# A two-layer hybrid attention trunk: probabilities turned square by square on VectorE, and sums of log f formed by scans

## The chip, the cores and the metric

The kernel runs on one core of one Trainium2 chip. The metric is the device time of one launch in microseconds (us). The kernel before was run three times: 934.83, 939.86 and 940.43 us, median 939.86 us. One further execution was profiled; all durations below are of that one.

## The reference

The input x is 256 rows of 2048 numbers in fp32. Each of two layers normalises x, multiplies it by one input projection, feeds four groups of four heads, gates each group, and adds an output projection to x. A last normalisation ends it.

```python
def hybrid_layer(x, l, ...):
    h = rms_norm(x, norm_g)
    p = split_columns(h @ w_in)
    log_f = log_sigmoid(p["fox_f"] + fox_fb)
    fox  = softmax(q k^T / sqrt(d) + F[t] - F[s]) v * silu(g)      # F = cumsum(log_f), causal
    diff = rms_norm((softmax(q1 k1^T) - lam * softmax(q2 k2^T)) v) * silu(g)
    moba = softmax(q k^T / sqrt(d)) v * silu(g)     # 256 rows are one block: plain causal attention
    a = log_sigmoid(p["gla_a"] @ wa2 + ba) / 16     # per head and channel
    gla  = rms_norm(o) * silu(g)                    # o_t = q_t S_t, S_t = diag(exp a_t) S_{t-1} + k_t^T v_t
    return x + concat(fox, diff, moba, gla) @ w_out
```

## The kernel before

**Projections.** All projections run on TensorE in fp32r with every operand split in a high and a low part (hi x hi, lo x hi, hi x lo), into the PSUM tiles `mm`. The weights come in 300 steps. A step loads a tile `raw` (128x1024, 512 KB, on SP's queue), ScalarE writes its high part `hi` and VectorE its low part `lo` (both line 183, `hi_of` and `lo_of`), and TensorE multiplies 12 times (line 285): 8 with `hi`, then 4 with `lo`. There are four buffers each of `raw`, `hi` and `lo`, and the builder prepares a step three steps ahead of its products (`ahead`, line 1249): the parts of step i+3 can be written when TensorE has left those of step i-1. Layer 0 has steps 0 to 119 of the input projection and 120 to 151 of the output projection; layer 1 likewise from 152. `hTp` is the turned, normalised x; `mTh` and `mTl` are the turned outputs of the groups, high and low. The output projection takes the groups in the order gla, fox, diff, moba, two steps each, so that its seventh and eighth step (126 and 127, 278 and 279) are the first to need moba.

**Side work.** Everything else is written as Python generators in a list of tasks (`tick`, line 266). After each step every task may go on to its next `yield`. `give_time` (line 1242) adds the step's TensorE time to a budget of VectorE and one of ScalarE, and `Costed` (line 171) charges each of their instructions a fixed cost and a cost per element. While either budget is overdrawn, no task goes on (line 270). When a step needs what no task has yet made, the tasks go on regardless, and the step's products are written behind what they wrote (line 1290). The order that results is fixed before the launch, and each engine runs its own list in order.

**Turned probabilities.** A softmax leaves its probabilities with the queries across the partitions: `p0`, four heads of 128x128 (first 128 queries), and `p1`, eight such squares (last 128 queries, two halves of keys). The product with the values needs them turned. `turned_p` (line 773) calls `turned` (line 292): two VectorE transposes write a tile `six` (128x1536), in which each 32x32 block is turned in place, and `moved` (line 305) sends it to DRAM (`turn`) by one DMA of POOL's queue and back by four, which puts the blocks where they belong. Five more turns of the task list are let pass (`LAND`). Fox and moba (`attend_columns`, line 791) read `six` directly; diff (line 905), where it is the stationary operand, first copies it to `z0` and `z1` on ScalarE. This happens six times: fox, diff and moba in two layers. All other tiles that are turned (queries, keys, gates, x) go the same way by `turned`.

**Sums of log f.** Gated linear attention (`gla`, line 622) needs exp of sums of log f over ranges of rows, for seven levels of halving and the two halves (NL + 1 = 8 sets of 128 columns, `ee`, tile `eight`). Log f is made with the rows across the partitions (`gl`), split in `gh` and `glo`, and multiplied by a constant 0/1 matrix divided by 16 (`a_r`, 128x1152): for each of two head pairs and two halves of rows, `a_r` gives a PSUM tile `pe`, of which ScalarE takes exp into `ee`. There are 10 products for each pair, 40 in all. Then come products of queries with `ee` (`tq`), of `ee` with keys, the score products `side<-tq,eight`, and masked copies.

Of the kernel before, what the change touches and what calls it, by code (L numbers as in the profile page):

```python
# [21 lines left out]
P = 128  # L22
# [4 lines left out]
H = 4  # L27
# [12 lines left out]
T2 = 5  # L40
T6 = 1
# [23 lines left out]
def _constants():  # L65
# [20 lines left out]
    sets, masks = [], []  # L86
    for h in GLA_LEVELS:
        blk, second = i // (2 * h), (i // h) % 2 == 1
        ref = blk * 2 * h + h - 1
        u, t = i[:, None], i[None, :]  # L90
        a = np.where(second[None, :], (u > ref[None, :]) & (u <= t), (u > t) & (u <= ref[None, :]))
        sets.append(a / GLA_TAU)
        masks.append(((blk[:, None] == blk[None, :]) & ~second[:, None])[:, second])
    sets += [(i[:, None] > i[None, :]) / GLA_TAU, (i[:, None] <= i[None, :]) / GLA_TAU]
    put("sets", np.concatenate(sets, 1), "b")
# [117 lines left out]
def hybrid_trunk(  # L213
# [17 lines left out]
    v_ = Costed(nc.vector, 0.06, 1.05e-3)  # L231
# [15 lines left out]
    s6 = Slots(wk, "six", T6)  # L247
# [85 lines left out]
    a_r = cp.tile([P, (NL + 2) * P], F32R, name="a_r")  # L333
# [24 lines left out]
    def constants():  # L358
# [6 lines left out]
        for name in ("sets", "upto", "masks"):  # L365
# [12 lines left out]
        v_.tensor_copy(a_r, s[0])  # L378
        v_.tensor_copy(upto_r, s[1])
        v_.tensor_copy(masks.rearrange("p l t -> p (l t)"), s[2])  # L380
# [241 lines left out]
    def gla(l, an):  # L622
# [14 lines left out]
        gl = yield from s2.take([P, 2, 256])  # L637
        yield from log_sigmoid(gl.rearrange("p m e -> p (m e)"), al[:, :512], e)
# [18 lines left out]
        for pair in range(2):  # L657
            ee = yield from s8.take([P, 2, NL + 1, P])
            for m in range(2):
                pe = yield from take_side()  # L660
                for b in range(2):
                    for part in (gh, glo):
                        lhs = part[:, m, pair * P:(pair + 1) * P]
                        if b == 0:
                            matmul(pe[:, :512], lhs, a_r[:, 0:512], part is gh, part is glo)
                        elif m == 0:
                            matmul(pe[:, 512:], lhs, a_r[:, 512:1024], part is gh, part is glo)
                        else:
                            matmul(pe[:, 512:896], lhs, a_r[:, 512:896], part is gh, False)
                            matmul(pe[:, 896:], lhs, a_r[:, (NL + 1) * P:], False, part is glo)  # L670
# [3 lines left out]
            yield  # L674
# [19 lines left out]
            v_.tensor_mul(ee[:, 1, NL], ee[:, 1, NL], qv[:, 1])  # L694
            both = yield from take_both()
# [21 lines left out]
        s2.put(gh, glo)  # L717
# [55 lines left out]
    def turned_p(p0, p1, pool0=s2, slot0=None):  # L773

        def release():
            pool0.put(p0 if slot0 is None else slot0)
            s4.put(p1)

        return (yield from turned([p0, p1.rearrange("p h j s -> p (h j) s")], s6, release))

    def normalised(p0, p1, su):
# [7 lines left out]
        return (yield from turned_p(p0, p1))  # L789

    def attend_columns(l, gi, name, qT, kT, forget=None):
# [11 lines left out]
        for h in range(H):  # L803
            v0, v1 = vn[:, 0, h * P:(h + 1) * P], vn[:, 1, h * P:(h + 1) * P]
            matmul(o[:, h, :P], v0, t[:, :, h], True, True)
# [524 lines left out]
```

## Time and profile before

| | us |
|---|---|
| three runs | 934.83, 939.86, 940.43 |
| profiled execution | 932.37 |
| its span, from the first to the last instruction | 930.2 |
| TensorE busy in the span | 913.7 |
| VectorE busy | 577.4 |
| ScalarE busy | 505.3 |
| GpSimd busy | 104.0 |

The profile names engines PE (TensorE's products), PEld (its loads of stationary operands), DVE (VectorE), ACT (ScalarE), POOL (GpSimd) and SP. An fp32 product of 128x128 stands in it as two instructions, so 12 such products are a group of x24. Line 183 is the helper that charges the budgets and line 285 the helper that issues products: there the tiles tell what an instruction is. Numbers behind a tile's name tell buffers apart and are left out by the profile.

### The profile page before, as it was taken

To read this page: it belongs to the slowest core of one execution; us is meant where nothing else is said; L and a number is where in the kernel's file an instruction comes from. 1 tells how busy PE (TensorE), PEld (TensorE's weight loads), DVE (VectorE), ACT (ScalarE), POOL (GpSimd) and SP (SyncE) were. 2 spreads that over 40 slices of the span, in tenths; PEclk is the share of its full clock that TensorE was granted. 3 is DMA by queue.
4 is the path that set the end of the run, shared out by engine and by line. 5 is a ranking of instruction groups with operands and counts; after the bars stand their busy time and mean duration, and the time that the engine had idled before them with its cause. 6 is when DMAs were issued, how large, how long until landed. Compare 5 with 4: busy or idle time off the path is not lost.

```text
span 930.2 us, 12655 instructions
## 1 busy us (share of the span) xinstructions
PE 913.7 (98%) x4734; PEld 777.7 (84%) x4734; DVE 577.4 (62%) x782; ACT 505.3 (54%) x712; POOL 104.0 (11%) x174
## 2 busy tenths in 40 slices
PE   9999999999999999999999999999999999989996
PEld 7989888898888888788898888888878888868886
DVE  7663876674764576456845457866656655664563
ACT  7587654455644456455656566446355445744441
POOL 0010011210111122001200101012201112130000
PEclk9999999999999999999999999999999999999999
DMA  9766476787677768678856856578956887695652
GB/s 324 268 209 198 163 240 200 233 238 258 216 209 248 239 201 274 204 228 268 261 176 185 245 143 205 181 220 230 284 177 212 249 239 219 201 296 199 199 163 91
DMA packets 59407, 204.56 MB, mean 220 GB/s; under 512 B 8497, under 2 KB 8785, under 8 KB 59346
## 3 DMA queue, kind: packets, MB, share of 16 engines
q1 hardware_dynamic: 46048, 164.20, 55.5%
q0 software_dynamic: 11664, 37.76, 14.7%
q10 hardware_dynamic: 1634, 1.80, 0.6%
q8 instruction: 37, 0.61, 0.3%
q14 instruction: 24, 0.20, 0.1%
HBM read 183.80 MB, written 19.92 MB: 219 GB/s over the span
## 4 chain that ended last, share of the span: by engine, by line
PE 92%; DMA 4%; issue 2%; DVE 1%; ACT 1%; POOL 1%; POOLq 0%; DVEq 0%; SPq 0%; ACTq 0%
PE mm L285 82%; PE side L285 10%; DMA six<-turn 2%; DMA raw<-in_weights 1%; DMA four<-turn 1%; DVE lo L183 0%; DMA four<-in_xt 0%; ACT hi L183 0%; POOL six L312 0%; ACT four L183 0%; DVE xs L183 0%; POOL four L312 0%; PE side L289 0%; DVE four L183 0%; DVE hTp L183 0%
## 5 line engine op out<-in xcount | busy, mean ns | idle before, releaser
L183 DVE TENSOR_TENSOR lo<-raw,hi 128x1024 fp32r<-128x1024 f32 (+3 forms) x301 | 365.7, 1220 | 297.3 <-ACT hi L183 292.7
L183 ACT ACTIVATE hi<-raw 128x1024 fp32r<-128x1024 f32 (+3 forms) x301 | 316.8, 1059 | 366.3 <-PE mm L285 318.0
L285 PE MATMUL mm<-hi,hTp 128*128 128x512 f32 (+2 forms) x2048 | 465.4, 371 | 0.3 <-DVE hTp L183 0.3
L285 PEld LDWEIGHTS mm<-hi,hTp 128*128 128x128 f32 x2048 | 358.2, 188 | 66.2 <-issue 1.4
L285 PE MATMUL mm<-lo,hTp 128*128 128x512 f32 (+2 forms) x1024 | 249.8, 369 | 0.1
L285 PEld LDWEIGHTS mm<-lo,hTp 128*128 128x128 f32 x1024 | 181.1, 188 | 32.9 <-DVE lo L183 0.3
L285 PE MATMUL mm<-hi,mTh 128*128 128x512 f32 (+1 forms) x256 | 95.2, 377 | 0.0
L285 PE MATMUL mm<-hi,mTl 128*128 128x512 f32 (+1 forms) x256 | 95.0, 376 | 0.0
L285 PE MATMUL mm<-lo,mTh 128*128 128x512 f32 (+1 forms) x256 | 64.4, 376 | 0.0
L312 POOL DMA_DIRECT2D four<-turn x84 | 46.0, 554 | 108.5 <-DMA turn<-four 53.9
L285 PEld LDWEIGHTS mm<-hi,mTl 128*128 128x128 f32 x256 | 48.2, 188 | 9.0 <-DVE mTl L183 0.3
L285 PEld LDWEIGHTS mm<-hi,mTh 128*128 128x128 f32 x256 | 48.2, 188 | 8.7
L285 PEld LDWEIGHTS mm<-lo,mTh 128*128 128x128 f32 x256 | 46.2, 188 | 8.8
L309 POOL DMA_DIRECT2D turn<-four x21 | 12.2, 582 | 324.3 <-DVE four L183 324.3
L183 ACT ACTIVATE four<-mm,rstd 128x512 f32<-128x512 f32 (+2 forms) x56 | 33.6, 647 | 3.6 <-DVE fx L183 3.5
L183 ACT ACT_TABLE_LOAD x26 | 33.4, 1283 | 3.3 <-DVE an L183 3.0
L285 PEld LDWEIGHTS side<-four,four 128*128 128x128 f32 (+1 forms) x256 | 26.0, 190 | 3.5 <-issue 1.4
L285 PE MATMUL side<-four,four 128*128 128x128 f32 (+1 forms) x256 | 27.7, 277 | 1.1 <-DMA four<-turn 1.1
L183 DVE STREAM_TRANSPOSE four<-four 128x1024 f32<-128x1024 f32 x18 | 22.3, 1241 | 0.3
L183 ACT ACTIVATE four<-side,nb 128x256 f32<-128x256 f32 (+1 forms) x48 | 20.4, 434 | 1.2 <-DVE nb L183 1.2
L183 DVE COPY_PREDICATED four<-masks,side 128x128 f32<-128x128 uint8 x56 | 19.1, 341 | 1.8
L285 PE MATMUL side<-six,four 128*128 128x128 f32 x96 | 13.1, 301 | 5.4 <-DMA six<-turn 5.4
(146 smaller groups left out, 540.5 us busy)
## 6 DMA issues: line engine op xcount, KB each, us to landing
raw<-in_weights SPq DMA_DIRECT2D x272, 512.0 KB, 4.2
turn<-four POOLq DMA_DIRECT2D x21, 512.0 KB, 4.8
four<-turn POOLq DMA_DIRECT2D x84, 128.0 KB, 4.9
raw<-in_weights SPq DMA_DIRECT2D x16, 516.0 KB, 4.8
raw<-in_weights SPq DMA_DIRECT2D x15, 528.0 KB, 5.0
turn<-six POOLq DMA_DIRECT2D x6, 768.0 KB, 4.5
six<-turn POOLq DMA_DIRECT2D x24, 192.0 KB, 6.6
turn<-gate POOLq DMA_DIRECT2D x4, 512.0 KB, 4.4
```

Of the source, the lines that this page charges most:

```text
L183: return f(*args, **kw)
L285: t_.matmul(out, lhsT, rhs, start=start, stop=stop)
L309: g_.dma_start(via, t.rearrange("p c a b -> p c (a b)"))
L312: g_.dma_start(t[c * 32:(c + 1) * 32].rearrange("p q a b -> p q (a b)"), via[:, c].rearrange("(q i) e -> i q e", q=4))
```

## The change

- `turned_p` no longer goes over DRAM. It writes a fixed tile `pT` (128 x 12 squares x 128) by VectorE transposes that read 32 partitions and write 32 others: for each of four target strips, four source strips, a transpose of `p0` (32 x 4 x 32) and one of `p1` (32 x 8 x 32). Where the source lies above the diagonal, only the second key half of `p1` is not zero there, and one transpose of 32x4x32 is left. That makes 10 of 32x8x32 and 16 of 32x4x32 for each turn, in four portions with a `yield` behind each. `pT` is zeroed once; a turn waits until the products of the one before it have been written.
- `attend_columns` and `diff` read `pT`; the ScalarE copies to `z0` and `z1` are gone. The pool `six` is gone.
- In `gla`, log f is made with head channels across the partitions (the two operands of `side<-wa,at` change places). Four scans (`cum`) for each layer give the running sum. For each pair, seven subtractions of 128x256 give the sum of each row less that of its block's reference row, one subtraction and one copy of 128x128 the last set. ScalarE takes their absolute value and then exp with the scale -1/16, both 128x1024, for each half of rows. The 40 products with `a_r`, the split in `gh` and `glo`, the PSUM tiles `pe` and the constant `a_r` with its load and its cast are gone. A `yield` is added ahead of the score products.
- The charge for a VectorE instruction goes from 0.06 + 1.05 n/1000 to 0.16 + 1.04 n/1000 us (n: elements in a partition).
- The pool `two` (2 KB in a partition) has seven buffers in place of five.

```diff
-T2 = 5
-T6 = 1
+T2 = 7
...
-    v_ = Costed(nc.vector, 0.06, 1.05e-3)
+    v_ = Costed(nc.vector, 0.16, 1.04e-3)
...
-        for m in range(2):
-            matmul(al[:, m * 256:(m + 1) * 256], at17[:, m * P:(m + 1) * P], wa[:, l], True, True)
+        for pair in range(2):
+            matmul(al[:, pair * SEQ:(pair + 1) * SEQ], wa[:, l, pair * P:(pair + 1) * P], at17, True, True)
...
-        gh = yield from s2.take([P, 2, 256], F32R)
-        hi_of(gh, gl)
-        yield
-        glo = yield from s2.take([P, 2, 256], F32R)
-        lo_of(glo, gl, gh)
+        cum = yield from s2.take([P, 2, SEQ])
+        for pair in range(2):
+            for m in range(2):
+                c = slice(m * P, (m + 1) * P)
+                v_.tensor_tensor_scan(cum[:, pair, c], gl[:, pair, c], gl[:, pair, c], 0.0, op0=OP.add, op1=OP.bypass)
...
+            for i, h in enumerate(GLA_LEVELS):
+                src = cum[:, pair].rearrange("p (m b w) -> p m b w", m=2, w=2 * h)
+                v_.tensor_sub(ee[:, :, i].rearrange("p m (b w) -> p m b w", w=2 * h), src,
+                              src[:, :, :, h - 1:h].to_broadcast([P, 2, 64 // h, 2 * h]))
+                if i == 3:
+                    yield
+            v_.tensor_scalar(ee[:, 0, NL], cum[:, pair, :P], cum[:, pair, P - 1:P], None, op0=OP.subtract)
+            v_.tensor_copy(ee[:, 1, NL], cum[:, pair, P:])
+            yield
             for m in range(2):
-                pe = yield from take_side()
...
+                a_.activation(ee[:, m], ee[:, m], AF.Abs)
+                a_.activation(ee[:, m], ee[:, m], AF.Exp, scale=-1.0 / GLA_TAU)
                 yield
-                a_.activation(ee[:, m].rearrange("p l t -> p (l t)"), pe, AF.Exp)
-                side.put(pe)
...
+    def turned_p(p0, p1):
+        while env["pT"] is None:
+            yield
+        t, env["pT"] = env["pT"], None
+        low = p1.rearrange("p h j s -> p (h j) s")
+        for s in range(4):
+            for q in range(4):
+                to, at = slice(s * 32, s * 32 + 32), slice(q * 32, q * 32 + 32)
+                if q < s:
+                    v_.transpose(t[to, H:3 * H:2, at], low[at, 0:2 * H:2, to])
+                else:
+                    v_.transpose(t[to, 0:H, at], p0[at, :, to])
+                    v_.transpose(t[to, H:3 * H, at], low[at, :, to])
+            yield
+        return t
```

How the order of instructions moves is shown at three places; each list is of one engine, in its order.

TensorE in layer 0, in the block of columns of `fox_v` (128x258), where the first set of sums stood. Before (`a_r` is the constant matrix, `two_732` and `two_752` are `gh` and `glo`):

```order
L285 MATMUL mm<-hi,hTp 128x258 x16
L285 MATMUL mm<-lo,hTp 128x258 x8
L285 MATMUL side_916<-a_r,two_732 128x512
L285 MATMUL side_916<-a_r,two_752 128x512
L285 MATMUL side_916<-a_r,two_732 128x512
L285 MATMUL side_916<-a_r,two_752 128x512
L285 MATMUL mm<-hi,hTp 128x258 x16
L285 MATMUL mm<-lo,hTp 128x258 x8
```

and now:

```order
L277 MATMUL mm<-hi,hTp 128x258 x16
L277 MATMUL mm<-lo,hTp 128x258 x8
L277 MATMUL mm<-hi,hTp 128x258 x16
L277 MATMUL mm<-lo,hTp 128x258 x8
L277 MATMUL mm<-hi,hTp 128x512 x8
L277 MATMUL mm<-lo,hTp 128x512 x4
```

The sums' products have left the list, here and at seven more places; nothing takes their place.

VectorE at the end of layer 0's input projection, from moba's turn to its gating. Before (`six_3184` is the tile of turned blocks, `four_3356` the gated result of moba, each `lo` the low part of one step's weights, three or four steps ahead of its products):

```order
L183 STREAM_TRANSPOSE six_3184<-two_3061 128x4x4x32
L183 STREAM_TRANSPOSE six_3184<-four_3089 128x8x4x32
L183 TENSOR_TENSOR lo<-raw,hi 128x1024 x2
L183 TENSOR_TENSOR mTl<-four_3182,mTh 128x1024
L183 TENSOR_TENSOR lo<-raw,hi 128x1024 x6
L183 TENSOR_TENSOR four_3356<-side_3325,gate_3137 128x4x8x32
L183 TENSOR_TENSOR lo<-raw,hi 128x1024 x2
L183 TENSOR_TENSOR mTl<-four_3356,mTh 128x1024
L183 TENSOR_TENSOR lo<-raw,hi 128x1024 x9
```

and now, from the middle of the third of the turn's four portions on:

```order
L176 STREAM_TRANSPOSE pT<-four_3116 32x8x32
L176 STREAM_TRANSPOSE pT<-two_3088 32x4x32
L176 STREAM_TRANSPOSE pT<-four_3116 32x8x32
L176 TENSOR_TENSOR lo<-raw,hi 128x1024
L176 STREAM_TRANSPOSE pT<-four_3116 32x4x32 x3
L176 STREAM_TRANSPOSE pT<-two_3088 32x4x32
L176 STREAM_TRANSPOSE pT<-four_3116 32x8x32
L176 TENSOR_TENSOR lo<-raw,hi 128x1024 x6
L176 TENSOR_TENSOR four_3442<-side_3429,gate_3164 128x4x8x32
L176 TENSOR_TENSOR mTl<-four_3442,mTh 128x1024
L176 TENSOR_TENSOR lo<-raw,hi 128x1024 x8
```

Before, six steps lay between the low part of diff (`mTl<-four_3182`) and moba's gating, and two more between gating and moba's low part; now gating and low part stand side by side, with no step between. On TensorE, moba's product with the values stood behind the third step of the output projection, three steps ahead of the first that needs moba; it now stands behind the sixth, right ahead of it. Layer 1 shows the same.

ScalarE in layer 1, at the exponentials of the first pair of gated linear attention. Before (`eight_4677` is `ee`, `side_4678` and `side_4709` are the sums in PSUM, `fe` belongs to the forget gate of fox):

```order
L183 ACTIVATE hi<-raw 128x1024 x2
L183 ACTIVATE four_4689<-mm,rstd 128x254 x2
L183 ACT_TABLE_LOAD
L183 ACTIVATE eight_4677<-side_4678 128x1024
L183 ACTIVATE hi<-raw 128x1024
L183 ACTIVATE eight_4677<-side_4709 128x1024
L183 ACTIVATE fe<-fx 128x8
L183 ACTIVATE fe<-fe 128x8
L183 ACT_TABLE_LOAD
L183 ACTIVATE fe<-fe 128x8
L183 ACTIVATE hi<-raw 128x1024 x2
```

and now:

```order
L176 ACTIVATE hi<-raw 128x1024
L176 ACTIVATE eight_4722<-eight_4722 128x1024
L176 ACT_TABLE_LOAD
L176 ACTIVATE eight_4722<-eight_4722 128x1024
L176 ACTIVATE fe<-fx 128x8
L176 ACTIVATE fe<-fe 128x8
L176 ACT_TABLE_LOAD
L176 ACTIVATE fe<-fe 128x8
L176 ACTIVATE hi<-raw 128x1024
L176 ACTIVATE eight_4722<-eight_4722 128x1024
L176 ACT_TABLE_LOAD
L176 ACTIVATE eight_4722<-eight_4722 128x1024
L176 ACTIVATE hi<-raw 128x1024 x5
```

Two absolute values and one more load of a table stand between the same copies of weights. The list as a whole has 25 loads of tables, where it had 27.

## Rows read from the trace of the kernel before

**Rows 1.** The first part of the page: busy time of each engine, its share of the span, and its instructions.

```profile
PE 913.7 (98%) x4734; PEld 777.7 (84%) x4734; DVE 577.4 (62%) x782; ACT 505.3 (54%) x712; POOL 104.0 (11%) x174
```

**Rows 2.** The chain of waits that ended last, over the whole span: its shares by engine and line.

```profile
by line: PE mm L285 81.6%; PE side L285 10.0%; issue 1.8%; DMA six<-turn 1.6%; DMA raw<-in_weights 1.3%; DMA four<-turn 0.6%; DVE lo L183 0.5%; DMA four<-in_xt 0.4%; ACT hi L183 0.3%; POOL six L312 0.3%; ACT four L183 0.2%; DVE xs L183 0.2%
```

**Rows 3.** TensorE in order of time, at the three places in the middle of the span where it stood still. Columns: start, duration (us), engine, line, operation, tiles, shape, count, and in brackets the idle time before with what ended it.

```profile
378.70 2.92 PE L285 MATMUL side<-six,four 128*128 128x128 f32 x24 [1.29 <-DMA six<-turn]
...
677.01 1.13 PE L285 MATMUL side<-four,four 64*128 64x128 f32 x14 [1.09 <-DMA four<-turn]
...
837.00 4.54 PE L285 MATMUL side<-six,four 128*128 128x128 f32 x24 [4.12 <-DMA six<-turn]
```

**Rows 4.** Pieces of the chain of waits in order of time (start, us, what): a product of probabilities and values that waited for nothing, and the two that stand at the end of each layer with what each waited for last.

```profile
260.46 2.68 PE side L285 x24
...
372.00 6.56 DMA six<-turn
...
378.70 2.92 PE side L285 x24
...
829.00 7.87 DMA six<-turn
...
837.00 4.54 PE side L285 x24
```

**Rows 5.** Stretches around the two waits at the ends of the layers: busy time of each engine with its instructions, granted TensorE clock, share of the DMA engines, GB/s.

```profile
377.50:382.00 4.50, 3.30 (x27) 3.25 (x28) 1.57 (x2) 0.10 (x1) 0.00 (x0) 1.00 1.00 398
833.00:837.00 4.00, 0.00 (x1) 0.03 (x1) 1.23 (x1) 0.07 (x1) 0.00 (x0) 1.00 1.02 267
837.00:842.00 5.00, 5.00 (x27) 4.92 (x28) 0.42 (x1) 0.00 (x0) 0.00 (x0) 0.66 1.02 401
```

**Rows 6.** TensorE's pieces of the chain in order of time (start, us, what): the sums of log f by products (x4 and x6), the first and the last two of the eight, and one step of projection (x12).

```profile
84.85 0.93 PE side L285 x4
...
88.64 0.99 PE side L285 x6
...
116.20 2.73 PE mm L285 x12
...
571.95 0.93 PE side L285 x4
...
575.61 0.99 PE side L285 x6
```

**Rows 7.** VectorE's groups of instructions, shapes kept apart: line, engine, operation, tiles, shapes, count, then busy us, mean ns of one, then the idle time before them with what ended it.

```profile
L183 DVE TENSOR_TENSOR lo<-raw,hi 128x1024 fp32r<-128x1024 f32 x268 | 325.9, 1221 | 271.6 <-ACT hi L183 267.1 <-PE mm L285 3.9
...
L183 DVE STREAM_TRANSPOSE four<-four 128x1024 f32<-128x1024 f32 x18 | 22.3, 1241 | 0.3
...
L183 DVE TENSOR_TENSOR tq<-eight,four 64x128 f32<-64x128 f32 x56 | 16.0, 286 | 0.6
...
L183 DVE TENSOR_TENSOR eight<-eight,four 128x128 f32<-128x128 f32 x36 | 7.9, 282 | 0.0
...
L183 DVE STREAM_TRANSPOSE six<-four 128x1024 f32<-128x1024 f32 x6 | 7.2, 1202 | 0.0
...
L183 DVE TENSOR_TENSOR two<-four,ct 128x256 f32<-128x256 f32 x8 | 3.3, 416 | 0.0
...
L183 DVE STREAM_TRANSPOSE six<-two 128x512 f32<-128x512 f32 x4 | 2.8, 704 | 0.0
...
L183 DVE TENSOR_SCALAR f<-f 128x8 f32<-128x8 f32 x2 | 0.3, 171 | 0.1
```

**Rows 8.** ScalarE's groups in the same form.

```profile
L183 ACT ACTIVATE hi<-raw 128x1024 fp32r<-128x1024 f32 x268 | 282.3, 1060 | 342.0 <-PE mm L285 303.9 <-DMA raw<-in_weights 10.6 <-DVE six L183 8.8
...
L183 ACT ACT_TABLE_LOAD x26 | 33.4, 1283 | 3.3 <-DVE an L183 3.0
...
L183 ACT ACTIVATE four<-four 128x1024 f32<-128x1024 f32 x10 | 10.5, 1052 | 0.3 <-DVE hTp L183 0.3
...
L183 ACT ACTIVATE eight<-side 128x1024 f32<-128x1024 f32 x8 | 8.2, 1023 | 0.9 <-PE side L285 0.8
...
L183 ACT ACTIVATE four<-six 128x1024 f32<-128x1024 f32 x2 | 2.1, 1043 | 0.0
...
L183 ACT ACTIVATE two<-six 128x512 f32<-128x512 f32 x2 | 1.3, 632 | 4.1 <-DMA six<-turn 4.1
...
L183 ACT ACTIVATE fe<-fe 128x8 f32<-128x8 f32 x4 | 0.8, 208 | 0.1
```

**Rows 9.** VectorE and ScalarE in order of time behind the product at 378.70 us (columns as in rows 3): gating the result, its high part, its low part.

```profile
381.65 1.23 DVE L183 TENSOR_TENSOR four<-side,gate 128x1024 f32<-128x1024 f32 x1 [2.80 <-PE side L285]
...
384.47 1.05 ACT L183 ACTIVATE mTh<-four 128x1024 fp32r<-128x1024 f32 x1
...
388.52 1.22 DVE L183 TENSOR_TENSOR mTl<-four,mTh 128x1024 fp32r<-128x1024 f32 x1
```

**Rows 10.** Pieces of the chain (start, us, what): the products of the first set of gated linear attention, in layer 0 and in layer 1.

```profile
103.33 3.12 PE side L285 x28
...
559.77 3.34 PE side L285 x28
```

**Rows 11.** The list of waits, one row: engine, line and tile that waited, for what; us in total, times, longest.

```profile
DVE lo L183 <- ACT hi L183: 292.7, 199, 5.2
```

**Rows 12.** The tile of turned probabilities: time from the issue of its DMAs to their landing.

```profile
DMA to landing us min/median/max: 4.1/6.4/9.2
```

More of the change, by code (lines that the diff above doesn't have):

```diff
@@ L85, in _constants @@
     put("neg", np.where(i[None, :] > i[:, None], NEG, 0.0), "b")
-    sets, masks = [], []
+    masks = []
     for h in GLA_LEVELS:
         blk, second = i // (2 * h), (i // h) % 2 == 1
[L89 to L92, printed above, removed]
         masks.append(((blk[:, None] == blk[None, :]) & ~second[:, None])[:, second])
-    sets += [(i[:, None] > i[None, :]) / GLA_TAU, (i[:, None] <= i[None, :]) / GLA_TAU]
-    put("sets", np.concatenate(sets, 1), "b")
     put("masks", np.concatenate(masks, 1), "b")
@@ L364, in constants @@
         s = []
-        for name in ("sets", "upto", "masks"):
+        for name in ("upto", "masks"):
             c, n = CAT[name]
@@ L377, in constants @@
         yield
-        v_.tensor_copy(a_r, s[0])
-        v_.tensor_copy(upto_r, s[1])
-        v_.tensor_copy(masks.rearrange("p l t -> p (l t)"), s[2])
+        v_.tensor_copy(upto_r, s[0])
+        v_.tensor_copy(masks.rearrange("p l t -> p (l t)"), s[1])
         v_.tensor_scalar(ones_r, ident, 0.0, 1.0, op0=OP.mult, op1=OP.add)
@@ L632, in gla @@
         al = yield from take_side()
-        for m in range(2):
-            matmul(al[:, m * 256:(m + 1) * 256], at17[:, m * P:(m + 1) * P], wa[:, l], True, True)
+        for pair in range(2):
+            matmul(al[:, pair * SEQ:(pair + 1) * SEQ], wa[:, l, pair * P:(pair + 1) * P], at17, True, True)
         yield
         e = yield from s2.take([P, 512])
-        gl = yield from s2.take([P, 2, 256])
-        yield from log_sigmoid(gl.rearrange("p m e -> p (m e)"), al[:, :512], e)
+        gl = yield from s2.take([P, 2, SEQ])
+        yield from log_sigmoid(gl.rearrange("p x t -> p (x t)"), al[:, :512], e)
         s2.put(e)
@@ L658, in gla @@
             ee = yield from s8.take([P, 2, NL + 1, P])
-            for m in range(2):
-                pe = yield from take_side()
[L661 to L670, printed above, removed]
+            for i, h in enumerate(GLA_LEVELS):
[7 more added lines that the diff above has]
+            yield
+            for m in range(2):
+                a_.activation(ee[:, m], ee[:, m], AF.Abs)
+                a_.activation(ee[:, m], ee[:, m], AF.Exp, scale=-1.0 / GLA_TAU)
                 yield
-                a_.activation(ee[:, m].rearrange("p l t -> p (l t)"), pe, AF.Exp)
-                side.put(pe)
-            yield
             def half(z, h, second):
@@ L771, in softmax @@
         return p
[L773 to L779, printed above, removed]
+    def turned_p(p0, p1):
[11 more added lines that the diff above has]
+                    v_.transpose(t[to, H:3 * H, at], low[at, :, to])
+            yield
+        return t
     def normalised(p0, p1, su):
@@ L788, in normalised @@
         yield
-        return (yield from turned_p(p0, p1))
+        t = yield from turned_p(p0, p1)
+        s2.put(p0)
+        s4.put(p1)
+        return t
     def attend_columns(l, gi, name, qT, kT, forget=None):
@@ L979, in diff @@
         s4.put(p1[1])
-        t = yield from turned_p(p0[:, 0], p1[0], s4, p0)
-        z0 = yield from s2.take([P, H, P])
-        z1 = yield from s4.take([P, 2 * H, P])
-        for z, part in ((z0, t[:, :, :H]), (z1, t[:, :, H:])):
-            a_.activation(z.rearrange("p n (q j) -> p n q j", q=4), part.rearrange("p q n j -> p n q j"), AF.Copy)
-        s6.put(t)
+        z = yield from turned_p(p0[:, 0], p1[0])
+        s4.put(p0, p1[0])
         yield
@@ L1278, in hybrid_trunk @@
     g_.memset(tq, 0.0)
+    env["pT"] = cp.tile([P, 3 * H, P], F32, name="pT")
+    g_.memset(env["pT"], 0.0)
     tasks += [constants()]
```

22 lines of the change are left out of this document (10 added, 12 removed).

## The prediction

> **What bounds the kernel now.** I read the busy times first: TensorE works 98% of the span, VectorE 62%, ScalarE 54% [rows 1]. The chain of waits says the same with an order to it: 91.6% of the span is TensorE's products, `mm` and `side` [rows 2]. So a microsecond counts only if TensorE executes it or stands still for it. TensorE in order of time shows three places in the middle of the span where it stood still: 1.29 us and 4.12 us ahead of moba's product with the values, at the end of layer 0 and of layer 1, and 1.09 us ahead of a product of diff in layer 1 [rows 3]. All three ended with a DMA of the trip over DRAM; the chain shows 6.56 and 7.87 us of such a DMA right ahead of the first two [rows 4]. VectorE and ScalarE matter only where TensorE waits for them: VectorE's `lo` stood 292.7 us waiting for ScalarE's `hi` [rows 11], and `hi` in turn waits for TensorE to leave a buffer [rows 8].
>
> **Sums of log f: TensorE's part.** Eight groups of products with `a_r` go, four of 0.93 us and four of 0.99 us [rows 6]: 4 x 0.93 + 4 x 0.99 = 7.7 us. All of it is on the path, since TensorE did not wait there and the order shows nothing in their place. The products that change operands keep their columns, and I cost that at nothing: at 0.22 us for 128 columns in fp32 (12 products in 2.68 us [rows 4]) all four make 1.8 us, so that even a change by a fifth would be 0.4 us.
>
> **Sums of log f: the other engines.** VectorE gets 28 subtractions of 128x256 at about 0.42 us and 8 small ones of 128x128 at about 0.28 us [rows 7], 14 us in all, and 8 scans of 128x128. No scan is in the trace; from below it is a plain operation of this shape, 0.28 us, from above a whole 128x1024, 1.22 us [rows 7]. I take 0.4 us, near the row of the same shape; all eight make 2 to 10 us, and lie in steps with room. The Trainium skill (DVE: opcode table, instruction layouts, handler registers and perf-mode slots, section Datapath and trigger behaviour) says the scan runs at half throughput, which by its rule would be an estimate of about 0.4 us too; no row here shows it. ScalarE gets 16 instructions of 128x1024 at 1.05 us and loses 8 at 1.02 us, the copies of diff (2 x 1.04 + 2 x 0.63 us) and two loads of tables at 1.28 us [rows 8]: +2.7 us. Neither engine is near its limit over the span, so this counts only where a burst of it comes late.
>
> One such burst is on the path: the first pair in layer 1. Counted from the end of the TensorE step behind which the first subtractions stand, VectorE ends its last one after about 4.3 us (two `lo`, seven subtractions, two small ones and what fox's gate takes between, 6.9 us, begun 2.6 us ahead of that point, when a buffer came free). On ScalarE then follow, by the order, an absolute value, a table, an exp, three short ones, a table, a copy, an absolute value, a table, an exp and a copy: 4 x 1.05 + 2 x 1.06 + 3 x 1.28 + 3 x 0.21 = 10.8 us [rows 8]. Behind that VectorE does three `lo`, 14 products of 0.29 us, two short ones and the first product of `ee` with keys: 3 x 1.22 + 4.0 + 0.34 + 0.28 = 8.3 us [rows 7]. Together 23.4 us, while TensorE needs eight steps of 2.73 us = 21.8 us [rows 6] to come to the score products. It waits about 1.5 us. The kernel before was already at this edge: the same products took 3.34 us in layer 1 against 3.12 us in layer 0 [rows 10]. Bounds: 0 and 4 us. In the other three pairs the same count leaves VectorE ahead or level, since fewer tables or more steps lie between.
>
> **Squares: what goes.** The trip over DRAM goes, 6 x 5 DMAs on POOL's queue, and with it both waits of TensorE for it. Layer 0: 1.29 us, and the product behind took 2.92 us against 2.68 us where nothing was late [rows 3, 4]: 1.5 us. Layer 1: 4.12 + 4.54 - 2.68 = 6.0 us; the longer product has its reason in the clock, granted at 0.66 from 837 to 842 us and at 1.00 behind the shorter wait [rows 5]. The 1.09 us of diff was a wait for the turn of its keys, whose DMAs stood behind those of fox's turn in POOL's queue; that queue is now empty there, and in VectorE's order 15 steps lie between transpose and the use of the product, where there were 9. I take 1.1 us back.
>
> **Squares: what comes.** A square transpose of part of the lanes is not in the trace. By whole ones, 1.20 us for 1024 elements and 0.70 us for 512 [rows 7], an element costs 1 ns and an instruction 0.2 us, so 128 elements make 0.32 us and 256 make 0.45 us. That lanes left idle do not shorten it, the products on 64 partitions show: 0.286 us, against 0.282 us on 128 [rows 7]. A turn is 16 x 0.32 + 10 x 0.45 = 9.6 us in place of 1.9 us. From below it is 26 of the smallest instruction, 0.17 us, 4.4 us; from above 26 whole transposes of 1.24 us, 32 us [rows 7]. Six turns add 46 us to VectorE, in stretches that had room. Beside a turn stand `lo`, 1.22 us in each step of 2.73 us: 1.5 us are free in each of the six steps over which a turn is spread, and since the parts are made three steps ahead a `lo` may be some 8 us late before TensorE misses it. I cost the turn itself at nothing; if that cover is gone, see the rivals.
>
> **The new wait.** The order has moba's product right ahead of the first step that needs its result. So TensorE waits out gating, high part and low part: 1.23 + 1.05 + 1.22 us [rows 9], with about 0.1 us of handing on and the same to start again, less the one product with `mTh` that can run before `mTl` is there, 0.2 us: 3.5 us in each layer. Nothing delays VectorE or ScalarE there, since their next step's parts are done during moba's product of 2.68 us [rows 4]. Before, three steps, 8 us, covered this. Queued behind the waiting TensorE are steps 126 on; ScalarE and VectorE wait for their buffers and lose the same time, which nobody else needs. Bounds: 2.3 us (if the low part were early) and 5.4 us (with the loss of clock of layer 1, 4.54 - 2.68 = 1.9 us [rows 4]). I take 3.5 us without that loss, as the wait is shorter than 4.12 us and broken by a product.
>
> The Trainium skill (TensorE: Matmul & The Clock Gate, section HAM oscillation) warns that a gap in TensorE's work, if long enough, drops its clock to half. The trace agrees at 4.12 us and shows nothing of it at 1.29 us; 3.5 us lies between. That result is the second rival.
>
> **The sum.** Span 930.2 - 7.7 - 1.5 - 6.0 - 1.1 + 2 x 3.5 + 1.5 = 922.4 us. The profiled execution took 932.37 us, 2.2 us more than its span: 924.6 us. The three runs lay 2.5 to 8.1 us over the profiled execution, the median 7.5 us. What can vary so in a program bound by TensorE are its waits for DMAs: those for `six` landed in 4.1 to 9.2 us [rows 12], at the one place with 1.29 us of waiting, at the other with 4.12 us and a slow clock. I take it that a little over half of the 7.5 us goes with them, as the starting loads still vary: 924.6 + 3 = 927.5 us, 1.3% under the median before. About 1% is what a measurement of this kernel can tell from no change.
>
> **Rivals.**
> - *The clock falls at both new waits.* For it: 0.66 behind 4.12 us [rows 5]. Against: the shorter wait, and the product within it. 1.9 us each: 931.3 us.
> - *The runs stay as far over the profile as they were.* For it: loads at the start are untouched, and the DMA engines are busy all through. Against: the two waits at moba ended with the trip that goes, and the third place has 15 steps now for its trip. 924.6 + 7.5 = 932 us, within 1%.
> - *VectorE falls behind (the slower side).* One mechanism at six places: the turn's squares are dearer than I take them, and TensorE waits for `lo`. In the nine steps around diff's turn VectorE has about 18 us of other work (nine `lo`, the scaling of diff's maps, a rotation with its transpose) in 24.5 us; with the 8 us that a `lo` may be late, a turn of up to 14.5 us is hidden, 0.56 us a square. At fox and moba, with 8.5 us of other work in six steps, it is 16 us. Above, all of it lands on TensorE: at 0.75 us a square, 19.5 us a turn, 2 x 5 + 4 x 3.5 = 24 us, so 951 us; at 0.9 us some 975 us. Slower than before it is from 0.68 us. Against: all rows of small instructions stand at 0.17 to 0.29 us [rows 7].
> - *More is gained:* the waits at moba at their lower bound and none in layer 1's first pair: 922 us.
>
> **Chances.** Forecast 0.48, clock 0.16, runs 0.16, VectorE 0.11, more 0.09. Faster by over 1% (under 930.5 us) are seven eighths of the forecast, most of the last and a fifth of the clock: 0.54. Slower by over 1% is VectorE's case: 0.11. The rest, 0.35, is within 1%. The range goes from 918 us (all bounds in favour, the runs close to the profile) to 941 us (clock and runs together, or the mildest case of VectorE). The likeliest case alone spans 923 to 932 us.
>
> **What would show it.** Right: no group with `a_r`, and TensorE's products shorter by 7.7 us; ahead of steps 126 and 278 idle time of 2.3 us and then 1.2 us, ended by ScalarE's `mTh` and VectorE's `mTl`, at a clock of 1.00; no wait of TensorE for a DMA behind the start; squares at 0.3 to 0.45 us; a wait of 1 to 2 us at layer 1's first score products. Wrong: TensorE waiting for `lo` during a turn; squares over 0.56 us; a clock below 1.00 behind the two gaps; or a median as far over the profile as it was.

## The result, and the profile after

The changed kernel takes 926.12 us (median of four runs, 925.78 to 927.91) against 939.98 us of the kernel before in the same session (four runs, 934.83 to 940.43). The ratio is 0.9855, with a 95% interval of 0.9806 to 0.9903: faster, by 1.0 to 1.9%. The profiled execution took 925.78 us with a span of 924.0 us and a mean granted clock of 0.994; before it was 932.37, 930.2 and 0.996. So the two profiles differ by 6.2 us of span, and the medians by 13.9 us. Both differences have to be explained.

The page's busy times, which answer to [rows 1], and its chain of waits by engine, which answers to [rows 2]:

```profile
PE 907.0 (98%) x4694; PEld 771.5 (83%) x4694; DVE 625.6 (68%) x967; ACT 506.4 (55%) x712; POOL 88.9 (10%) x145
...
PE 95%; DVE 2%; ACT 1%; issue 1%; DMA 0%; POOLq 0%; POOL 0%; DVEq 0%; SPq 0%; ACTq 0%
```

TensorE has 40 products fewer and is busy 6.7 us less; VectorE is busy 48 us more. DMA, 4% of the chain before, is down to 0%; VectorE's share went from 1% to 2%. TensorE in order of time shows where it stands still now (columns as in [rows 3]):

```profile
386.71 0.51 PE L277 MATMUL mm<-hi,mTh 128*128 128x512 f32 x1 [2.40 <-ACT mTh L176]
387.97 0.80 PE L277 MATMUL mm<-hi,mTl 128*128 128x512 f32 x1 [0.76 <-DVE mTl L176]
...
563.47 3.39 PE L277 MATMUL side<-tq,eight 128*128 128x128 f32 x28 [0.76 <-DVE eight L176]
...
840.85 0.50 PE L277 MATMUL mm<-hi,mTh 128*128 128x512 f32 x1 [2.41 <-ACT mTh L176]
842.11 0.79 PE L277 MATMUL mm<-hi,mTl 128*128 128x512 f32 x1 [0.76 <-DVE mTl L176]
```

The three waits for DMAs of [rows 3] are gone. New are the two breaks ahead of steps 126 and 278, each in two parts with one product between them, and a wait for `eight` in layer 1's first GLA pair. The chain over the first break (start, us, what), which answers to [rows 4, 9]:

```profile
381.63 2.69 PE side L277 x24
384.32 0.02 issue
384.35 1.23 DVE four L176
385.58 0.02 issue
385.60 1.06 ACT mTh L176
386.67 0.02 issue
386.69 1.24 DVE mTl L176
387.93 0.04 issue
```

From the end of moba's product at 384.32 to the product with `mTl` at 387.97 are 3.65 us. One product lies within, which takes 0.23 us where products follow each other, so 3.4 us are lost. Behind each break the clock falls; these stretches (columns as in [rows 5]) cover the break and the 6 us after it:

```profile
382.00:388.00 6.00, 2.84 (x23) 2.33 (x21) 3.53 (x3) 1.06 (x1) 0.00 (x0) 0.96 0.49 167
388.00:394.00 6.00, 6.00 (x20) 4.89 (x21) 1.23 (x1) 1.06 (x1) 0.00 (x0) 0.75 0.01 3
836.00:842.00 6.00, 2.95 (x23) 2.44 (x22) 3.61 (x3) 1.06 (x1) 0.00 (x0) 0.96 0.49 160
842.00:848.00 6.00, 5.89 (x20) 4.76 (x21) 1.28 (x2) 1.06 (x1) 0.00 (x0) 0.76 0.01 3
```

A mean of 0.75 over 6 us with TensorE busy throughout means that 25% of 6 us, 1.5 us, are lost: about half of that stretch ran at 1.2 GHz and half at 2.4 GHz. The second fall costs 1.4 us. VectorE's new instructions, in the form of [rows 7]:

```profile
L176 DVE STREAM_TRANSPOSE pT<-four 32x256 f32<-32x256 f32 x60 | 23.6, 394 | 0.0
...
L176 DVE STREAM_TRANSPOSE pT<-four 32x128 f32<-32x128 f32 x56 | 17.0, 303 | 1.0
...
L176 DVE STREAM_TRANSPOSE pT<-two 32x128 f32<-32x128 f32 x40 | 12.1, 302 | 0.5
...
L176 DVE TENSOR_TENSOR eight<-two 128x256 f32<-128x256 f32 x28 | 10.0, 417 | 0.0
...
L176 DVE TENSOR_TENSOR_SCAN two<-two 128x128 f32<-128x128 f32 x8 | 2.7, 404 | 0.0
```

A turn of 16 squares at 0.303 us and 10 at 0.394 us is 8.8 us.

### The profile page after: what moved, and what is told of

Its sections match the earlier page's. It is cut to its first block, busy times and chain, and to the rows that moved or that the text cites. A ratio compares the mean times of both kernels' runs of the same rounds, so it can differ in the third digit from the quotient of the medians.

```text
span 924.0 us, 12695 instructions
## 1 busy us (share of the span) xinstructions
PE 907.0 (98%) x4694; PEld 771.5 (83%) x4694; DVE 625.6 (68%) x967; ACT 506.4 (55%) x712; POOL 88.9 (10%) x145
## 4 chain that ended last, share of the span: by engine, by line
PE 95%; DVE 2%; ACT 1%; issue 1%; DMA 0%; POOLq 0%; POOL 0%; DVEq 0%; SPq 0%; ACTq 0%
PE mm L277 86%; PE side L277 9%; ACT eight L176 0%; DMA four<-in_xt 0%; DVE tq L176 0%; DVE lo L176 0%; ACT hi L176 0%; DVE mTl L176 0%; DVE four L176 0%; ACT mTh L176 0%; DVE xs L176 0%; ACT L176 0%; PE side L281 0%; DVE hTp L176 0%; POOLq L1324 0%
## 5 line engine op out<-in xcount | busy, mean ns | idle before, releaser
L277 PE MATMUL mm<-hi,mTl 128*128 128x512 f32 (+1 forms) x256 | 97.0, 383 | 1.5 <-DVE mTl L176 1.5
L277 PEld LDWEIGHTS mm<-hi,mTl 128*128 128x128 f32 x256 | 49.2, 192 | 11.2 <-DVE mTl L176 2.1
L176 DVE STREAM_TRANSPOSE pT<-four 32x128 f32<-32x128 f32 (+1 forms) x116 | 39.3, 350 | 1.0
L277 PEld LDWEIGHTS side<-four,four 128*128 128x128 f32 (+1 forms) x224 | 22.0, 190 | 2.3 <-issue 1.4
L277 PE MATMUL side<-four,four 128*128 128x128 f32 (+1 forms) x224 | 23.3, 277 | 0.0
```

The source lines that it names most:

```text
L176: return f(*args, **kw)
L277: t_.matmul(out, lhsT, rhs, start=start, stop=stop)
```

## The experiments

| Run | Median us (range, runs) | Ratio to before, 95% | Profiled: span, clock |
|---|---|---|---|
| e1 scans only | 926.46 (924.08–928.02, 6) | 0.9853 [0.9817, 0.9888] | 922.3, 0.996 |
| e2 squares only, old charge | 929.92 (928.16–930.13, 6) | 0.9887 [0.9853, 0.9921] | 928.1, 0.995 |
| e3 changed, old charge | 924.40 (922.96–925.08, 6) | 0.9829 [0.9792, 0.9866] | 922.9, 0.993 |
| e4 changed, squares uncharged | 915.87 (915.75–916.41, 6) | 0.9743 [0.9710, 0.9776] | 914.0, 0.998 |
| e5 before, again | 938.72 (1) | – | 936.6, 0.993 |
| e6 as e4, product held back | 927.65 (927.28–928.20, 4) | 0.9868 [0.9809, 0.9926] | 926.1, 0.991 |
| e7 changed, squares twice | 935.06 (933.92–935.93, 10) | 0.9966 [0.9940, 0.9991] | 932.1, 0.994 |
| e8 squares only, uncharged | 922.91 (922.79–923.63, 4) | 0.9819 [0.9771, 0.9867] | 921.0, 0.997 |
| e9 changed, no absolute values | 925.31 (1) | – | 923.5, 0.994 |
| e10 budget only | 933.80 (930.80–935.46, 10) | 0.9951 [0.9923, 0.9980] | 933.4, 0.993 |
| e11 scans only, again | 925.76 (1) | – | 924.0, 0.996 |
| e12 before, third | 944.03 (1) | – | 941.9, 0.989 |

**What makes the two breaks: e4, e3, e6.** e4 leaves the squares and the other transposes out of the budget:

```diff
-                    v_.transpose(...)
+                    nc.vector.transpose(...)
```

> The changed kernel with its budget, but the squares (and the other transposes) not charged; moba's product with v stands behind step 121 (273). VectorE has then 8.8 us of squares, 4 lo and one mTl, some 15 us, from the end of the normalising on (356.3 us in the changed kernel's trace), that is until about 371.3, and TensorE comes to that place at about 370.6. Theory A: a wait of TensorE for the last square of 0.7 us (0 to 2) at each moba, in place of the 5.1 us of break and slow clock: median about 917.5. Rival B (nothing waits, VectorE being further ahead than this reckoning): as with the old charge, 916. Rival C (uncharged work delays the lo pieces: TensorE waits for lo by what the budget doesn't see): 921 or more.

Measured: 915.87 us, no break, a clock of 1.00 there. Theory A's wait of 0.7 us for the last square did not come, since the squares end at 369.6 us and the product starts at 370.65 us; rival B's 916 is met. Moba's product stands four steps earlier than in the changed kernel, and gating, high part and low part of layer 0 lie under those steps. VectorE and ScalarE of e4 in order of time:

```profile
374.20 1.22 DVE L176 TENSOR_TENSOR four<-side,gate 128x1024 f32<-128x1024 f32 x1
376.33 1.05 ACT L176 ACTIVATE mTh<-four 128x1024 fp32r<-128x1024 f32 x1
...
380.36 1.22 DVE L176 TENSOR_TENSOR mTl<-four,mTh 128x1024 fp32r<-128x1024 f32 x1
```

The three take 7.4 us here, not 3.5, because each is written a step later than the one it needs, behind the `hi` or `lo` of that step. That is what e3 fell over:

```diff
-    v_ = Costed(nc.vector, 0.16, 1.04e-3)
+    v_ = Costed(nc.vector, 0.06, 1.05e-3)
```

> The changed kernel with VectorE's budget as before (0.06 and 1.05e-3 a piece); moba's product with v then stands behind step 123 (275) instead of 125 (277). Theory A (the new breaks are the budget's placing, not the squares): both breaks go, 2 x 3.65, and with them the stretch at half clock behind each, 2 x 1.5: 10.3 us less than the changed kernel, span about 913.7, execution about 915.5, median about 916. Rival B (the higher budget was needed: with the lower one more is written ahead of the lo pieces, and TensorE waits for lo): several waits of TensorE or its weight loads for lo, together 3 us or more, median 919 or above. Rival C (the break goes, the slow clock has another cause): 918.5.

Measured: 924.40 us, 8 us above theory A. The product stands two steps ahead, and that is not enough. All engines of e3 in order of time:

```profile
378.74 1.23 DVE L176 TENSOR_TENSOR four<-side,gate 128x1024 f32<-128x1024 f32 x1 [0.73 <-PE side L277]
...
381.53 1.04 ACT L176 ACTIVATE mTh<-four 128x1024 fp32r<-128x1024 f32 x1
...
384.43 1.23 DVE L176 TENSOR_TENSOR lo<-raw,hi 128x1024 fp32r<-128x1024 f32 x1 [1.54 <-ACT hi L176]
385.57 1.22 DVE L176 TENSOR_TENSOR mTl<-four,mTh 128x1024 fp32r<-128x1024 f32 x1
...
386.84 0.50 PE L277 MATMUL mm<-hi,mTl 128*128 128x512 f32 x1 [2.46 <-DVE mTl L176]
```

`mTh` is done at 382.57, but `mTl` stands on VectorE behind a `lo` that waits for its `hi` until 384.4. TensorE stands 2.46 us, and the granted clock is 0.72 over the 6 us from 386 and from 840. So theory A (no break) and rival C (no break, but the slow clock) are both wrong: with two steps of lead a break is left. Rival B's time (919 or above) is met, but TensorE waits for `mTl` and not for `lo`. e6 isolates the place of the product, with e4's charges:

```diff
+        while name == "moba" and env["i"] < 125 + 152 * l:
+            yield
         ops = yield from take_side()
...
+        env["i"] = i
```

> The kernel with uncharged squares (915.9 us), in which moba's product with v is held until behind step 125 (277), where the changed kernel has it; nothing else moves. Theory A (the place of this product alone makes the 10 us between the changed kernel and that one): both breaks of 3.65 us come back with the slow clock behind them, median about 925 to 926. Rival B (the charge does more than place it, for instance in the fox and diff stages): 919 to 922.

Measured: 927.65 us, waits of 2.4 and 0.76 us in both layers as in the changed kernel. The place alone makes the whole difference to e4. The clock stayed low for longer here: 0.50 over all of 388 to 394 us, so 3 us are lost behind the first break in these 6 us alone, where the changed kernel lost 1.5; that is why the median lies above theory A's 925 to 926.

**The parts alone: e2, e8, e1, e10.** e2 and e8 are the kernel before with `turned_p`, its callers and `pT` of the change; e2 charges the squares by the old budget, e8 charges neither them nor the other transposes.

> The kernel before, with the squares alone; the a_r products, the budget and the two-buffers (5) are those of before. moba's product with v then stands behind step 123 (275), two steps of 2.72 us ahead of the out product that needs it. Theory A: the DMA waits go (-1.5 and -6.0, -1.1 for the waiting keys of diff), and the 3.65 us of gating, mTh and mTl lie under two steps: no new break, no slow clock. Span about 921.6, execution about 923.8, and the timed runs come within 1 us of it: median about 924. Rival B (the excess is not of the trips): runs 3 to 8 us over the profile, median about 930. Rival C (the squares themselves open the new break, whatever the budget): two breaks of 3.65 us with 1.5 us of slow clock each, execution about 934.

> The kernel before with the squares alone, not charged; moba's product with v stands behind step 121 (273), as in the kernel with scans and uncharged squares, and no break should be left. Theory A (the two parts add up): 930.2 - 1.5 - 6.0 - 1.1 = 921.6 of span, execution about 923.5, that is 7.7 us above the kernel that has the scans as well; median 923 to 924. Rival B (the parts don't add: the scans are worth less or more once no break is left): 919 or less, or 927 or more.

e2 measured 929.92 us: two breaks of 2.46 us, by the same `mTl` as in e3, which theory A had not seen. Rival B's median of 930 is met, but not its reason: the runs lie around their profile and not 3 to 8 us over it. e8, without break, measured 922.91 us, just under theory A's 923 to 924. Against e4, which has the scans besides (and the new charge, and two more buffers of `two`), it is 7.0 us longer: with the 0.75 us that the scans bring back as a wait in e4, the `a_r` products were worth 7.8 us. The two parts add up.

e2 shows one more thing, in TensorE's granted clock behind two breaks of the same 2.46 us:

```profile
390.90 0.50 PE L283 MATMUL mm<-hi,mTl 128*128 128x512 f32 x1 [2.46 <-DVE mTl L182]
...
845.97 0.50 PE L283 MATMUL mm<-hi,mTl 128*128 128x512 f32 x1 [2.46 <-DVE mTl L182]
```

The stretches behind them (columns as in [rows 5]):

```profile
390.00:396.00 6.00, 5.09 (x22) 4.24 (x23) 2.08 (x2) 1.46 (x2) 0.00 (x0) 1.00 0.27 87
845.00:851.00 6.00, 5.03 (x15) 3.99 (x16) 1.48 (x2) 1.06 (x1) 0.00 (x0) 0.72 0.31 90
```

e1 has the scans alone:

> The kernel before, with the scans and differences alone; probabilities still go over DRAM, the budget and the buffers are those of before. Theory A (each part of the change is worth what its own stage shows, and the excess of the runs over their profile comes from the two trips of moba's probabilities): the eight groups of a_r products go, -7.7 us; the first GLA pair of layer 1 waits about 0.8 us as in the changed kernel; the DMA waits at moba stay (1.3 and 4.1 us, the second with a slow clock behind it). Span about 923.3, execution about 925.5; the timed runs still lie 2 to 8 us over it and differ by several us: median about 932. Rival B (the excess belongs to the GLA stage that is taken out here): runs within 1 us of the profile, median about 926. Rival C (the scans cost time that the new budget alone hides): execution 929 or more.

Measured: a profile of 922.3 us (theory A: 923.3), but a median of 926.46 us, as rival B had it, though its runs spread up to 3.9 us over their profile and not within 1 us. The median lies 2.4 us over the profile, where that of before, in the same session, lay 7.8 us over the first profile of before. So most of the excess went with the scans alone, though the trips over DRAM stayed. e10 has the budget alone:

```diff
-    v_ = Costed(nc.vector, 0.06, 1.05e-3)
+    v_ = Costed(nc.vector, 0.16, 1.04e-3)
```

> The kernel before, with VectorE's budget alone as in the changed kernel (0.16 and 1.04e-3 a piece). The GLA products stand one to four steps later, moba's product with v behind the same step as before (122, 274). Theory A (the budget moves the time only through the place of moba's product): no difference beyond the spread of the runs of before, median 937 to 942. Rival B (the later writing takes VectorE's work out of the way of the lo pieces, or lets TensorE wait in the GLA stage): 5 us or more to either side.

Measured: 933.80 us, 4.4 us less than the 938.2 us of before in that session; theory A's 937 to 942 is missed. Neither e1's profile nor e10's shows a wait for the turned keys of diff any more.

**Where the excess stood: e5, e12, e11.** These are the kernel before, twice, and e1 again, each for its profile.

> The kernel before, unchanged, once more with a profile. Its runs lie 2 to 13 us over the one profile there is, and have granted clocks from 0.986 to 0.995: the span times one minus the clock is 13.2 us in the longest and 4.7 us in the shortest, the rest of the span 928 to 932 us in all of them. Theory A (the excess is slow clock behind the waits at moba): this execution shows the two DMA waits of TensorE (1.3 and 4.1 us, a little longer or shorter) and windows under 0.8 behind both of them, where the first profile had one behind the second alone. Rival B: the low clock stands somewhere else, in the GLA stage with the a_r products.

> The kernel before, unchanged, a third profile. Theory A: the longer its span, the more of it stands at the four places: moba in layer 0 with its product, the keys in layer 1, moba in layer 1 with its product; what is left of the span is the same within 1 us as in the other two profiles (930.2 and 936.6 us, of which these places take 14.5 and 20.7 us: 1.29 + 2.92 + 1.09 + 4.12 + 4.54 + 0.5 for the split records, and 3.22 + 4.42 + 2.83 + 4.32 + 5.46 + 0.5). Rival B: the difference stands elsewhere by 2 us or more.

> The kernel with the scans alone, unchanged, once more with a profile. Its runs came 13.7 us under those of before where 7.7 us of products went. Theory A (the rest lies at the waits for trips over DRAM: the two profiles of before show 1.3 and 3.2 us at moba in layer 0 and 1.1 and 2.8 us for the turned keys in layer 1, the one of this kernel 1.2 and none): this execution shows again no wait for the keys, and under 2 us at moba in layer 0 with a clock of 1.00 behind it; span 922 to 926. Rival B (the waits vary here as much as there, and the difference is made elsewhere): a wait of 2.5 us or more in layer 0 or one for the keys, with a span still under 927.

TensorE of e5 in order of time, to be held against [rows 3]:

```profile
380.55 4.42 PE L285 MATMUL side<-six,four 128*128 128x128 f32 x24 [3.22 <-DMA six<-turn]
...
679.16 0.46 PE L285 MATMUL side<-four,four 64*128 64x128 f32 x2 [0.32 <-DMA four<-turn]
...
682.13 1.13 PE L285 MATMUL side<-four,four 64*128 64x128 f32 x14 [2.51 <-DMA four<-turn]
...
842.32 5.46 PE L285 MATMUL side<-six,four 128*128 128x128 f32 x24 [4.32 <-DMA six<-turn]
```

of e12:

```profile
380.83 4.54 PE L285 MATMUL side<-six,four 128*128 128x128 f32 x24 [3.51 <-DMA six<-turn]
...
680.67 0.46 PE L285 MATMUL side<-four,four 64*128 64x128 f32 x2 [1.38 <-DMA four<-turn]
...
683.90 2.04 PE L285 MATMUL side<-four,four 64*128 64x128 f32 x14 [2.78 <-DMA four<-turn]
...
848.38 4.83 PE L285 MATMUL side<-six,four 128*128 128x128 f32 x24 [6.43 <-DMA six<-turn]
```

and of e11:

```profile
375.68 2.92 PE L279 MATMUL side<-six,four 128*128 128x128 f32 x24 [1.61 <-DMA six<-turn]
...
561.17 3.39 PE L279 MATMUL side<-tq,eight 128*128 128x128 f32 x28 [0.84 <-DVE eight L177]
...
830.76 4.48 PE L279 MATMUL side<-six,four 128*128 128x128 f32 x24 [5.41 <-DMA six<-turn]
```

Against the first profile of before, e5 is 6.4 us longer. Moba in layer 0 waits 1.93 us more, and its product takes 1.50 us more, with a slow clock (0.72 over 380 to 386 us) behind the longer wait; the keys wait 1.74 us more; moba in layer 1 waits 0.20 us more and its product takes 0.92 us more: 6.3 us. e12 is 11.7 us longer: 2.22 + 1.62 + 3.07 + 0.91 + 2.31 + 0.29 = 10.4 us at the same places; the rest is slow clock that reaches past these products (0.54 over 683 to 689 us, behind the keys' waits), and with it the expectation's 1 us for all else is just missed. So in these three profiles the excess is waits for trips over DRAM that vary from one execution to the next, and slow clock behind them. e1 and e11 show 1.2 and 1.6 us at moba in layer 0 at full clock, and no wait for the keys. In layer 1 they wait as before.

**The squares' cover: e7.**

```diff
-                    v_.transpose(t[to, 0:H, at], p0[at, :, to])
+                    for f in (v_, nc.vector):
+                        f.transpose(t[to, 0:H, at], p0[at, :, to])
```

and the same for the other squares.

> The changed kernel with each of the 26 squares of a turn written twice, the second time uncharged, so that nothing else moves: 8.8 us more of VectorE in each of the six turns. Theory A (the slack that the changed kernel's trace shows between the last square and the product that reads them: 9.2 to 9.8 us at moba, 9.8 to 10 at diff, over 30 at fox): all of it stays hidden, at most 1 us each, median 926 to 928. Rival B (the slack that the prediction counted from the kernel before: covered up to 0.56 us a square at diff and 0.61 at fox and moba, where two writes come to 0.68): 3.0 us at each diff, 1.7 at each fox and moba, 12.8 in all, median about 939. Rival C (the lo pieces queue behind the squares and TensorE waits for lo): over 940.

Measured: 935.06 us, 8.9 above the changed kernel, between A and B. TensorE of e7 in order of time, layer 0:

```profile
367.53 1.19 PE L277 MATMUL mm<-lo,mTh 128*128 128x512 f32 x4 [0.53 <-DVE lo L176]
...
380.28 1.19 PE L277 MATMUL mm<-lo,mTh 128*128 128x512 f32 x4 [1.40 <-DVE lo L176]
...
390.65 0.50 PE L277 MATMUL mm<-hi,mTh 128*128 128x512 f32 x1 [3.75 <-ACT mTh L176]
391.91 0.50 PE L277 MATMUL mm<-hi,mTl 128*128 128x512 f32 x1 [0.76 <-DVE mTl L176]
```

TensorE never waits for the last square. At moba it waits for `lo` (0.53 + 1.40 us in each layer, rival C's mechanism), and the break becomes 1.1 to 1.35 us longer, together 6.3 of the 8.1 us by which the span grew; at fox and diff nothing waits at all.

**The wait in layer 1's first GLA pair: e9.** The absolute values are left out, so the decays come from signed differences.

```diff
-                a_.activation(ee[:, m], ee[:, m], AF.Abs)
+                a_.us += 0.22 + 0.88e-3 * 1024
```

> The changed kernel without the absolute values in the GLA stage (16 fewer of 1.055 us on ScalarE, still charged to its budget; the decays are then computed from signed differences, so the output is another). Nothing else moves. Theory A (the 0.76 us wait for eight in the first GLA pair of layer 1 is the end of a ScalarE burst of two absolute values, two exponentials and their table loads, some 10 us, in whose chain VectorE stands): with two absolute values of 1.05 us less before them, the products find their eight ready, the wait is gone, and the rest of the trace is that of the changed kernel: 925.1 us. Rival B (VectorE's own row of products and lo pieces, busy from 556.3 to 563.5 without a gap, sets the end): the wait stays at 0.5 to 0.8, 925.8.

Measured: a span of 923.5 us, 0.5 less, and no wait for `eight`. Theory A holds: VectorE's row ends in time if ScalarE's burst ends 2.1 us sooner.

e9 shows one more thing. Its break in layer 1 has the same two parts as in the changed kernel, and no slow clock follows. TensorE in order of time:

```profile
841.65 0.50 PE L277 MATMUL mm<-hi,mTh 128*128 128x512 f32 x1 [2.41 <-ACT mTh L176]
842.91 0.50 PE L277 MATMUL mm<-hi,mTl 128*128 128x512 f32 x1 [0.76 <-DVE mTl L176]
```

The stretch behind it (columns as in [rows 5]):

```profile
843.00:849.00 6.00, 6.00 (x27) 4.92 (x28) 1.50 (x2) 2.12 (x2) 0.00 (x0) 1.00 0.15 29
```

In layer 0 the clock is 0.50 over 388 to 394 us, as in e6.

## Why the prediction was right, step by step

The forecast was 927.5 us, measured were 926.12 us. The terms of the span, as predicted and as the traces have them:

| Term | Predicted us | Measured us |
|---|---|---|
| `a_r` products | -7.7 | -7.8 (e8 against e4) |
| DMA waits at moba, with slow clock | -7.5 | -7.5, all gone |
| Keys of diff | -1.1 | -1.1, gone |
| Two new breaks | +7.0 | +6.8 |
| Clock behind the breaks | 0 | +2.9 |
| Layer 1's first GLA pair | +1.5 | +0.8 |
| Sum | -7.8 | -5.9 (span: -6.2) |

*Sums of log f* were right in both parts; the wait on the path was there, at half its size. The scan's 0.404 us met the 0.4 us taken. Beside the 0.28 us of a plain operation of this shape, it agrees with the half throughput that the Trainium skill (DVE: opcode table, instruction layouts, handler registers and perf-mode slots, section Datapath and trigger behaviour) states for it.

*The new wait* was right in place, mechanism and size (3.4 us each for 3.5). Where the prediction said "without that loss, as the wait is shorter than 4.12 us and broken by a product", it was wrong: the clock fell behind both breaks, for 1.5 and 1.4 us, against the rival's 1.9. Neither reason was enough: a break of this form was followed by a fall at five of six places (changed kernel, e6, e9), in spite of its product. In e2 and e3 an unbroken 2.46 us was followed by a fall at three of four places, in e5 3.22 us by one and the 2.51 us at the keys by none (1.00 over 682 to 688 us). Waits of 1.2 to 1.7 us at moba in layer 0 were followed by none. So at breaks of 2.4 to 2.5 us the fall came in some places and not in others, and where the break had two parts it cost 0 to 3 us; what decides it is not shown. The prediction cited the Trainium skill (TensorE: Matmul & The Clock Gate, section HAM oscillation), by which a long enough gap in TensorE's work drops its clock to half. The changed kernel's trace agrees with it, with 0.75 and 0.76 over the 6 us behind the breaks; layer 1 of e9, with 1.00 behind the same break, does not.

*The runs over the profile.* The prediction kept 3 of 7.5 us, as "the starting loads still vary". The median lies 0.3 us over the profile; e5 and e12 show that what varied were the waits at moba and at the keys of diff, and the change removes all of them. This error of 2.7 us and the 2.9 us of the clock have opposite signs, so it is luck that the total is closer than its terms. The prediction named only moba for the excess; the keys of diff took up to 4.2 us of a run.

*The keys' reason*, fox's turn ahead of them in POOL's queue, fits the queue's order, though no run changes that order alone. POOL in order of time, before:

```profile
659.60 0.56 POOL L309 DMA_DIRECT2D turn<-four  x1
670.01 2.18 POOL L312 DMA_DIRECT2D four<-turn  x4 [9.86 <-PE mm L285]
```

and in e1:

```profile
648.68 0.56 POOL L303 DMA_DIRECT2D turn<-four  x1 [11.51 <-DVE four L177]
651.53 0.55 POOL L303 DMA_DIRECT2D turn<-six  x1 [2.30 <-DVE six L177]
...
659.80 2.18 POOL L306 DMA_DIRECT2D four<-turn  x4
```

Before, VectorE has turned the keys at 655.7 us, and their write to DRAM (`turn<-four`) is issued right behind the reads of fox's turn. In e1, as in e11, it stands ahead of fox's write, and the reads are issued 11.2 us ahead of the product that needs them. Before, that product began, after its wait, 7.0 us behind the issue of the reads. In e10 the order is that of before and the wait is gone all the same: the product stands one step, 2.7 us, later (as in e1 and e11), and begins 8.8 us behind the issue. Against e5's profile, e10's is 3.2 us shorter: it has neither the 2.8 us of waiting at the keys nor 3.0 us of e5's wait and slow product at moba in layer 0, but more waiting and slow clock in layer 1. Why moba's trip in layer 0 was short in e1, e10 and e11 stays open, and with it a part of e10's 4.4 us.

*The squares* cost 8.8 us a turn for the 9.6 us predicted and stayed hidden. The slower rival's mechanism is real, as e7 shows, but its bound was wrong where it counted: at diff the prediction had 14.5 us of cover, and 17.6 us made no wait there. At moba it had 16 us and a price of 1.7 us beyond; 1.9 us of waiting for `lo` came, and 1.1 to 1.35 us of longer break.

*A slip in the rivals:* by the prediction's own terms, "more is gained" makes 927.5 - 2 x 1.2 - 1.5 = 923.6 us, not 922.

e4 beats both kernels: 915.87 us, 10.2 us under the changed one. What the change gave away at the two breaks is the place of moba's product, which the budget sets: right ahead of its use with 0.16 us an instruction, two steps ahead with 0.06, four with the transposes uncharged.

## What to carry to other kernels

Where a planner sets the order by costs, look at what a new price moves to the last place before its use: the chain behind it, here three short steps on two engines, is worth more than the instructions priced. Count the lead of such a chain in slots of the order, not in its busy time, since each link can stand behind a piece of the steps' own work on its engine. And profile a varying kernel more than once: the waits that make its runs vary can be small in the one execution that was looked at, and a slow clock can follow a wait in one execution and not in another.

## What the runs showed of the hardware

The same break of 2.46 us was followed by a clock of 1.00 in one layer and of 0.72 in the other (e2), and so was the break of 2.41 and 0.76 us around one product, by 0.50 and 1.00 (e9). The stretch at the lower clock lasted from some 3 us (the changed kernel) to 6 us or more (e6, 0.50 over 388 to 394). A transpose on 32 lanes cost 0.303 us for 128 elements and 0.394 us for 256, less than the 0.32 and 0.45 us that the whole ones gave by a straight line.
